# A 32-byte load from each row of the first block of b, put first on ScalarE's queue

## The chip, the cores and the metric

The kernel runs on one core of one Trainium2 chip. The metric is the device time of one execution in microseconds (us); the number given is the median over several runs. Five engines work side by side: TensorE (PE in the profile; PEld is its loading of weights), VectorE (DVE), ScalarE (ACT), GpSimd (POOL) and SyncE (SP). DMAs are issued by SP, ACT or POOL and carried out by 16 DMA engines.

## The reference

```python
def reference(a, b, c):            # a 1024x1024, b 1024x2048, c 2048x1024, float32
    h = np.matmul(a, b)
    h = 0.5 * h * (1 + np.tanh(np.sqrt(2 / np.pi) * (h + 0.044715 * h ** 3)))
    return np.matmul(h, c).astype(np.float32)
```

Two matrix products with a GELU (tanh form) between them.

## The kernel before

All loads are started at the beginning, and the whole schedule is written out by hand: each engine carries out its instructions in the order of the program text, and a tile's readers wait for its writers.

The first product needs `a` transposed. Parts of `a` and `b` come in two ways. SP's queue loads five pieces as float32 into staging tiles (`sta` for a, `stb` for b), lines 75 to 79; DVE and ACT then cast them to bf16 (`cast_a`, `cast_b`, lines 108 and 110). All the rest is loaded by POOL's queue, which casts on the way, lines 86 to 104. POOL's first load stands behind a small copy (line 81) that reads the first piece of `a`, so that it isn't issued before that piece has landed.

The five pieces on SP's queue, in order:

- line 75, `a_part(0, 0)`: rows 0 to 511 of a, columns 0 to 255, 512 KB, as 512 runs of 1,024 bytes. In what follows, a(0,0).
- line 76, `b_part(0)`: rows 0 to 255 of b, columns 0 to 511, 512 KB, as 256 runs of 2,048 bytes. Partition p gets row p and row p + 128. In what follows, b(0).
- line 77, `a_part(1, 0)`: rows 512 to 1023 of a, columns 0 to 255, 512 KB: a(1,0).
- line 78, `a_part(0, 1)`: rows 0 to 511 of a, columns 256 to 511, 512 KB: a(0,1).
- line 79: rows 256 to 383 of b, columns 0 to 511, 256 KB.

A row of b has 2,048 floats, so rows that follow each other lie 8 KB apart in memory; a row of a has 4 KB.

ScalarE's first work is a GELU on one column (line 82), which loads its function table. PE starts with products on a constant (`stir`, line 125), then turns the pieces of `a` with transposes (line 145, copied out by DVE in line 146 into `aT`), and computes the first 512 columns of h with plain products, block by block as the pieces arrive (`block`, line 114). While a(0,0) and b(0) are worked on, a(1,0) has to land, and so on.

From 24 us on, the other columns of h and the second product are made by the class `Seven`: a 2x2 scheme of Strassen and Winograd with seven products in place of eight (line 212), whose sums of operands are made by DVE (line 170) and whose results are collected by ACT (line 298) and DVE (line 303). The outputs are stored from SP's queue (line 429).

The tile `room`, 16 floats a partition, is allocated in line 55 and not used.

Of the kernel before, what the change touches and what calls it, by code (L numbers as in the profile page):

```python
# [9 lines left out]
F32 = mybir.dt.float32  # L10
# [9 lines left out]
def kernel(ctx, tc, a, b, c, out):  # L20
    nc = tc.nc
# [8 lines left out]
    bv = b.rearrange("(kt p) n -> p kt n", p=128)  # L30
# [3 lines left out]
    consts = ctx.enter_context(tc.tile_pool(name="consts", bufs=1))  # L34
# [17 lines left out]
    gate = consts.tile([128, 1], F32, name="gate")  # L52
    g = consts.tile([128, 1], F32, name="g")

    consts.tile([128, 16], F32, name="room")

    c_sb = keep.tile([128, NT, P], BF16, name="c_sb")
    hT = [keep.tile([128, NT, H], BF16, name=f"hT{h}") for h in range(2)]
# [10 lines left out]
    def a_part(h, q):  # L69
        return av[:, 4 * h:4 * h + 4, ds(q * 256, 256)]  # L70

    def b_part(q):
        return bv[:, 2 * q:2 * q + 2, 0:H]

    nc.sync.dma_start(out=sta[:, 0, 0], in_=a_part(0, 0))  # L75
    nc.sync.dma_start(out=stb[:, 0:2], in_=b_part(0))  # L76
    nc.sync.dma_start(out=sta[:, 1, 0], in_=a_part(1, 0))
# [21 lines left out]
    for n in range(2):  # L99
        for k in range(0, KT, 4):  # L100
            nc.gpsimd.dma_start(out=b2[:, k:k + 4, ts(n, H)],
                                in_=bv[:, k:k + 4, ds(1024 + n * H, H)])
# [385 lines left out]
```

## Time and profile before

| | us |
|---|---|
| median of 3 runs | 117.6 (117.41 to 117.97) |
| span of the profiled execution, first to last instruction | 115.7 |
| PE busy in it | 111.1 |
| DVE busy | 90.0 |
| ACT busy | 51.4 |

The profile is of one execution. Its span leaves out what lies before the first and after the last instruction; the time of a run has it in, which is why the median is 1.9 us longer than the span. The granted clock of TensorE was 1.00 throughout.

The DMA queues in the whole execution (packets, megabytes, and share of the time of the 16 engines): the rows of the queue that SP issues on (q1) and of POOL's (q0).

```profile
q0 software_dynamic: 8672, 9.31, 47.6%
q1 hardware_dynamic: 4736, 6.56, 15.8%
```

The issues on SP's queue at the start, from the timeline (start, length of the issue, queue, line, what is loaded). The length is the time that SP needs to issue, not the time of the transfer:

```profile
1.24 0.50 SPq L76 DMA_DIRECT2D stb<-in_b_dram  x1
1.78 0.46 SPq L77 DMA_DIRECT2D sta<-in_a_dram  x1
2.29 0.51 SPq L78 DMA_DIRECT2D sta<-in_a_dram  x1
2.83 0.55 SPq L79 DMA_DIRECT2D stb<-in_b_dram  x1
```

From issue to landing these loads take (median of each kind) 6.1 us for the three of `sta` and 5.3 us for line 76.

### The profile page before, as it was taken

Reading aid. Unit: us, or ns where it says so; the run is one execution under the profiler, and the core shown is the slowest. Engines: PE = TensorE matmul, PEld = TensorE weight load, DVE = VectorE, ACT = ScalarE, POOL = GpSimd, SP = SyncE. Lnnn points to the kernel's source line nnn. Section 1 sums busy time; section 2 is a strip of 40 time slices with the busy share of each in tenths; the row PEclk is TensorE's granted clock in tenths of the full one; section 3 lists DMA queues with packets and bytes.
Section 4 is the critical chain, followed back from the end, with each engine's and each line's share of the span. In section 5 each row is a group of like instructions: output and inputs, shape, how many; then the busy total and the mean of one; then the engine's idle time right before and its main releaser. Section 6 shows DMA issues by size and latency. Waiting matters only on the chain.

```text
span 115.7 us, 1461 instructions
## 1 busy us (share of the span) xinstructions
PE 111.1 (96%) x542; PEld 77.1 (67%) x542; DVE 90.0 (78%) x107; ACT 51.4 (44%) x86; POOL 17.2 (15%) x29
## 2 busy tenths in 40 slices
PE   7989999999999999999999999999999999999980
PEld 6645555546776447888885444688888888888860
DVE  0347748789999998935699999999999986954770
ACT  5053000999259997166698429500124982000000
POOL 2497755223322000000000000000000000000000
PEclk9999999999999999999999999999999999999999
DMA  2999999999999999998000000060000002014993
GB/s 69 295 381 229 200 199 205 204 208 205 206 211 209 212 213 209 212 210 168 8 0 0 6 0 0 38 235 0 0 0 0 0 4 91 1 73 176 370 363 106
DMA packets 13414, 15.94 MB, mean 138 GB/s; under 512 B 736, under 2 KB 9312, under 8 KB 13408
## 3 DMA queue, kind: packets, MB, share of 16 engines
q0 software_dynamic: 8672, 9.31, 47.6%
q1 hardware_dynamic: 4736, 6.56, 15.8%
q8 instruction: 4, 0.07, 0.3%
q14 instruction: 2, 0.02, 0.0%
HBM read 20.97 MB, written 4.19 MB: 218 GB/s over the span
## 4 chain that ended last, share of the span: by engine, by line
PE 90%; DMA 5%; SPq 1%; DVE 1%; issue 0%
PE ps L212 76%; PE ps L114 11%; DMA sta<-in_a_dram 5%; PE pt L145 3%; SPq L76 0%; DVE ab L110 0%; SPq L75 0%; DVE ot L375 0%
## 5 line engine op out<-in xcount | busy, mean ns | idle before, releaser
L212 PE MATMUL ps<-x,s 128*128 128x512 f32 x128 | 29.6, 391 | 0.0
L212 PEld LDWEIGHTS ps<-x,s 128*128 128x128 f32 x128 | 24.0, 188 | 5.1
L212 PE MATMUL ps<-x,x 128*128 128x512 f32 x96 | 22.9, 394 | 0.0
L212 PEld LDWEIGHTS ps<-x,x 128*128 128x128 f32 x96 | 18.0, 188 | 3.9
L114 PE MATMUL ps<-aT,b 128*128 128x512 bf16 x64 | 16.1, 379 | 0.2 <-DVE b L110 0.2
L298 ACT ACTIVATE v<-ps 128x512 f32<-128x512 f32 x10 | 6.0, 599 | 19.1 <-PE ps L212 19.1
L212 PE MATMUL ps<-c_sb,hT 128*128 128x512 bf16 (+1 forms) x72 | 14.2, 356 | 0.0
L212 PE MATMUL ps<-x 128*128 128x512 f32 x56 | 13.2, 392 | 0.0
L212 PEld LDWEIGHTS ps<-x 128*128 128x128 f32 x56 | 10.2, 188 | 2.6 <-ACT u L298 0.4
L118 ACT ACTIVATE hT<-ps 128x512 bf16<-128x512 f32 x14 | 7.3, 595 | 9.7 <-PE ps L114 9.7
L212 PEld LDWEIGHTS <-hT 128*128 128x128 bf16 x72 | 6.9, 98 | 7.0 <-issue 0.5
L118 ACT ACTIVATE hT<-ot 128x512 bf16<-128x512 f32 x18 | 10.4, 624 | 2.0 <-DVE ot L303 2.0
L212 PE MATMUL ps<-aT,b 128*128 128x512 bf16 x48 | 10.7, 379 | 0.0
L146 DVE COPY aT<-pt 128x512 bf16<-128x512 bf16 x16 | 6.7, 423 | 5.1 <-PE pt L145 5.1
L303 DVE TENSOR_TENSOR ot<-ps,u 128x512 f32<-128x512 f32 x10 | 6.7, 690 | 5.1 <-ACT u L298 5.1
L303 DVE TENSOR_TENSOR ot<-ps,v 128x512 f32<-128x512 f32 x10 | 6.7, 688 | 4.8 <-DMA out_dram<-ot 3.8
L170 DVE TENSOR_TENSOR x<-c_sb 128x1024 fp32r<-128x1024 bf16 x8 | 9.3, 1226 | 0.0
L114 PEld LDWEIGHTS <-b 128*128 128x128 bf16 x64 | 5.7, 98 | 4.5 <-DVE b L110 0.3
L212 PEld LDWEIGHTS <-b 128*128 128x128 bf16 x48 | 4.6, 98 | 5.7 <-issue 0.3
L104 POOL DMA_DIRECT2D c_sb<-in_c_dram x8 | 5.6, 702 | 13.1 <-DMA b<-in_b_dram 12.4
L170 DVE TENSOR_TENSOR x<-b 128x1024 fp32r<-128x1024 bf16 (+1 forms) x4 | 7.0, 1752 | 0.6 <-issue 0.6
L298 ACT ACTIVATE u<-ps 128x512 f32<-128x512 f32 x10 | 5.9, 598 | 3.4 <-PE ps L212 3.2
(44 smaller groups left out, 111.3 us busy)
## 6 DMA issues: line engine op xcount, KB each, us to landing
c_sb<-in_c_dram POOLq DMA_DIRECT2D x8, 512.0 KB, 20.0
out_dram<-ot SPq DMA_DIRECT2D x13, 256.0 KB, 2.1
b<-in_b_dram POOLq DMA_DIRECT2D x6, 512.0 KB, 15.3
sta<-in_a_dram SPq DMA_DIRECT2D x3, 512.0 KB, 6.1
abq<-in_a_dram POOLq DMA_DIRECT2D x5, 256.0 KB, 7.9
out_dram<-ot SPq DMA_DIRECT2D x6, 128.0 KB, 2.0
stb<-in_b_dram SPq DMA_DIRECT2D x1, 512.0 KB, 5.3
b<-in_b_dram POOLq DMA_DIRECT2D x2, 256.0 KB, 8.2
```

The costliest lines, as they stand in the source:

```text
L104: nc.gpsimd.dma_start(out=c_sb[:, t:t + 2], in_=cv[:, t:t + 2])
L114: nc.tensor.matmul(p, b1[:, k, ts(t, 128)], aT[:, h, k], start=(k == 0), stop=(k == KT - 1))
L118: nc.scalar.activation(hT[h][:, t], p, AF.Gelu_apprx_tanh)
L145: nc.tensor.transpose(pt[:, n, ts(m, 128)], ab[:, m, ts(n, 128)], ident)
L146: nc.vector.tensor_copy(aT[:, h, 2 * q + n], pt[:, n])
L170: nc.vector.tensor_tensor(out=dst[:, r], in0=x[:, r], in1=y[:, r], op=op)
L212: nc.tensor.matmul(p[:, ds(c0, w)], l[:, k, ts(j, 128)], r[:, k, ds(c0, w)], start=(start and k == 0), stop=(k == self.kt - 1), skip_group ...
L298: nc.scalar.activation(st, p, AF.Copy)
L303: nc.vector.tensor_tensor(out=ot, in0=p, in1=st, op=ADD)
```

## The change

`room` gets a name and the shape 128 x 2 x 8 in place of 128 x 16, the same 64 bytes a partition. One DMA is added ahead of the five on SP's queue in the text, on ScalarE's queue, where it is the first instruction. It reads the first 8 floats (32 bytes) of each of the rows 0 to 255 of b, partition p getting rows p and p + 128 as in `b_part(0)`. No instruction reads `room`. All other instructions stay as they are, in the same order on each engine; their line numbers go up by one.

```diff
-    consts.tile([128, 16], F32, name="room")
+    room = consts.tile([128, 2, 8], F32, name="room")
...
+    nc.scalar.dma_start(out=room, in_=bv[:, 0:2, 0:8])
     nc.sync.dma_start(out=sta[:, 0, 0], in_=a_part(0, 0))
     nc.sync.dma_start(out=stb[:, 0:2], in_=b_part(0))
     nc.sync.dma_start(out=sta[:, 1, 0], in_=a_part(1, 0))
```

## The prediction

> **What bounds the kernel now.** I read the chain of waits first, then its first 13 us piece by piece, then the timeline and a table by stretches of the same time, and last the single packets of the DMA queues.
>
> ```profile
> span 115.7 us, 1461 instructions
> PE 111.1 (96%) x542; PEld 77.1 (67%) x542; DVE 90.0 (78%) x107; ACT 51.4 (44%) x86; POOL 17.2 (15%) x29
> PE 90%; DMA 5%; SPq 1%; DVE 1%; issue 0%
> ```
>
> TensorE sets the end: 90% of the chain is PE, and PE runs from 8.38 us to 112.4 us with no gap. The only other large piece is a load, 5% of the span, and it lies at the start:
>
> ```profile
> 0.74 0.44 SPq L75
> 1.24 0.50 SPq L76
> 1.78 6.10 DMA sta<-in_a_dram
> 7.90 0.44 DVE ab L110
> 8.38 0.62 PE pt L145 x8
> ```
>
> This load is the third one on SP's queue, line 77 (I call it a(1,0)). It lands at 7.88 us; DVE and ACT cast it, PE turns it, and from there PE never stops. So the end stands at "landing of a(1,0)" plus work that does not depend on the change. The load waits 6.10 us because two others are ahead of it in the DMA engines: a(0,0) of line 75 and b(0) of line 76. That is where the change acts.
>
> ```profile
> 0.74 1.28 ACT L82 ACT_TABLE_LOAD   x1 [0.74 <-PEq L472]
> 2.03 0.20 ACT L82 ACTIVATE g<-const-float32-0.0 128x1 f32<-128x1 f32 x1
> 4.40 0.69 DVE L110 CAST ab<-sta 128x1024 bf16<-128x1024 f32 x1 [4.40 <-DMA sta<-in_a_dram]
> 6.54 0.94 ACT L108 ACTIVATE b<-stb 128x256 bf16<-128x256 f32 x2 [4.30 <-DMA stb<-in_b_dram]
> 7.90 0.43 DVE L110 CAST ab<-sta 128x512 bf16<-128x512 f32 x1 [0.67 <-DMA sta<-in_a_dram]
> ```
>
> The casts start when the loads land: a(0,0) at 4.38, b(0) at 6.51, a(1,0) at 7.88 us. Each load has 512 KB. b(0) takes 6.51 - 4.38 = 2.13 us, a(1,0) only 1.37 us. The table of stretches (columns: the stretch, its length, busy time of the five engines, granted clock, DMA share, GB/s) says the same:
>
> ```profile
> 0.00:1.85 1.85, 1.07 (x3) 0.92 (x4) 0.00 (x0) 1.11 (x1) 0.69 (x6) 1.00 0.00 1
> 1.85:3.60 1.75, 1.75 (x6) 1.39 (x5) 0.00 (x0) 0.38 (x2) 0.00 (x0) 1.00 0.83 262
> 3.60:5.60 2.00, 1.93 (x11) 1.34 (x10) 0.71 (x2) 0.00 (x0) 1.17 (x2) 1.00 0.91 265
> 5.60:7.10 1.50, 1.11 (x10) 0.76 (x10) 0.97 (x4) 0.56 (x2) 1.50 (x3) 1.00 1.07 363
> 7.10:8.40 1.30, 1.21 (x7) 0.36 (x6) 0.56 (x2) 0.87 (x2) 1.30 (x3) 1.00 1.09 386
> 8.40:9.20 0.80, 0.80 (x10) 0.64 (x11) 0.38 (x2) 0.13 (x1) 0.80 (x2) 1.00 1.07 378
> ```
>
> 265 GB/s while b(0) is read, 386 GB/s later, on the same queue. In the trace's packet records b(0) has 256 packets of 2,048 bytes, of mean length 114 ns, 86 of them stretched (over 92 ns, up to 405 ns). The 128 packets of the next load from b, line 79, take 84 ns each without one exception. b(0)'s excess over 84 ns is 7.8 us in all, 0.49 us for each of 16 engines. a(0,0) shows 34 stretched packets of 512 (2.8 us, 0.17 us an engine), a(1,0) shows 3. Between 5.6 and 5.85 us b(0)'s last packets are still stretched (187, 153, 145 ns) while a(1,0)'s beside them on other engines all take 46 ns. So the stretching belongs to b(0), not to that moment.
>
> **The change part by part.** Added: one DMA on ScalarE's queue, 128 x 2 x 8 floats, 256 pieces of 32 bytes from the rows that b(0) reads, with no reader. Nothing is removed. All else keeps its order on PE, DVE, POOL and SP; the tile `room` has the 64 bytes a partition that it had.
>
> Gain S, what b(0) saves. Lower bound 0: the touch warms nothing. Upper bound: b(0) runs at a(1,0)'s pace, 2.13 - 1.37 = 0.76 us. What decides is why b(0) is slow. For "first touch of this part of b": the clean next load from b has the same pitch of 8 KB between rows, and POOL's later loads of pairs of rows of b, which move 2,048 bytes read per 98 ns packet, show one slightly stretched packet among 810. Neither pitch nor pairs alone are slow later. Against it: lines 77 and 79 also touch new rows and are clean, so the cold thing must be larger than a row. With the touch in the same order, the engine that reads a row later touches it first, so I take the upper bound, S = 0.76.
>
> Cost T, the engines' time for the touch. 256 pieces over 16 engines are 16 packets each and one semaphore packet. No 32-byte packet is in the trace; the nearest row is the 4-byte semaphore packet of 9 ns, so 17 x 9 = 0.15 us an engine. Upper bound: all of b(0)'s excess moves into the touch, 0.15 + 0.49 = 0.64 us. Lower bound 0, since the engines are not full while a(0,0) begins: from 1.85 to 2.5 us 82 packets start, where 16 engines at a(1,0)'s pace (1.37 us for 32 packets each) would start 0.65 x 16 x 32 / 1.37 = 243; two thirds of 0.65 us, 0.43 us an engine, is empty. The touch is issued at the same moment as a(0,0) and falls into that hole. I take the middle of 0 and 0.15, T = 0.07; the cover is this hole, and without it T is 0.15 to 0.64.
>
> Cost D, a later first issue on SP. ACT and SP both start at 0.74 us. An issue on SP takes 0.44 to 0.55 us here. If the two don't share anything, or SP comes first, D = 0: b(0)'s own issue at 1.24 is over long before its first packet at 3.59 us, so half a microsecond there is hidden. If ACT's comes first and SP's must wait, a(0,0) and all behind it move by D = 0.44. The trace shows no two queues issuing at once. I take 0, and keep 0.44 for the range.
>
> The Trainium skill speaks against this: "Perfetto Trace Analysis", section "DMA Instruction — HWDGE (DVE, Sync)", says that the block that writes the descriptors is shared by two sequencers and locked by one at a time. No row here shows it; by that rule, with ScalarE first, D would be the 0.44 and my sum 117.35.
>
> ScalarE itself: the issue (0.44 to 0.55, as on SP) goes ahead of the table load of 1.28 us and the activation of 0.20 us, which then end near 2.8 instead of 2.23 us. ScalarE's next work is the cast of b at 6.54, or 5.8 if b(0) is faster; 3 us of idle time hide this. What would be late next without that cover is this cast, and PE's first products at 6.83 us.
>
> What follows behind a(1,0): a(0,1) and the last part of b are behind it on the same queue and move with it. POOL's queue comes next: its first DMA was issued at 5.08 to 5.95, but its packets begin at 9.01 us, and they begin engine by engine (3, 5, 22, 33 packets in the four tenths of a microsecond from 9.0), as the last packets of SP's queue leave (8.95 to 9.6 us). So it starts when SP's queue is drained, and moves too. If it didn't, PE would soon wait: the half of `abq` that lands at 15.84 is used at 16.09, so only 0.25 us of a gain would stay.
>
> Before b(0): if a(0,0) lands a little later by T, its cast (4.40 to 5.09), PE's turns (5.15) and DVE's copy (to 6.00) still end near b(0)'s new landing, 5.8; a(1,0) would land at 7.2 and still be last.
>
> Sum: -S + T + D = -0.76 + 0.07 + 0 = -0.69 us. The profiled execution has a span of 115.7 us; the median of the runs is 117.6 us, 1.9 us more, which lies around the span and which I leave as it is. So a span near 115.0, and 117.6 - 0.7 = 116.9 us.
>
> **The rivals.**
>
> (1) The stall only moves. The 256 touches pay what b(0) paid, ahead of a(0,0): T = 0.64, so -0.76 + 0.64 = -0.12, 117.5 us. For it: 0.49 us an engine has to be paid somewhere, if it is paid by row. Against it: the empty time in a(0,0)'s start, and the clean new rows of lines 77 and 79.
>
> (2) Slower: the stretch is not a matter of first touch. b(0)'s rows then read as slowly after the touch (S = 0), and the touch, on the same rows, stands ahead of a(0,0) with T = 0.15 to 0.64; in the middle 0.40, 118.0 us, and with D = 0.44 118.4 us. It decides from the point where T + D is more than S, that is, when less than T + D of the 0.76 us is saved. For it: the touch reads 32 of 2,048 bytes, and rows that lines 77 and 79 read for the first time are not slow at all. Against it: b's later loads are clean.
>
> (3) The gain is hidden: S is had, but POOL's queue starts by its own clock, and PE waits for `abq`: 0.25 us remain, 117.35 us. Against it: the hand-over engine by engine.
>
> **How the numbers follow.** The forecast has 0.48 (own range 116.6 to 117.3, from S = 0.76 with T up to 0.15, down by a tenth or two for what a(0,0) itself may save of its 0.17, up for a part of S), (1) 0.17, (2) 0.28, (3) 0.07. A measurement of this kernel can tell about 0.5%, 0.59 us, from no change: faster is below 117.0, slower above 118.2. Of the forecast 0.35 lie below 117.0, the rest above; (1) and (3) are within. Of (2) about 0.2 lie above 118.2 (with D, or with T near 0.64), the rest below; 0.06 more I give to slowdowns where (1) comes with D and with stretched packets in a(0,0). So faster 0.35, same 0.39, slower 0.26. The range goes from 116.6 to 118.4: below it lies S and all of a(0,0)'s stretching, above it more than T = 0.40 with D.
>
> **What would show it.** Right: b(0)'s packets at 84 ns, the casts on `stb` near 5.8 us, the one on `sta` that starts PE near 7.2 us, POOL's first packets near 8.3 us, and the rest of PE moved as one block. S is wrong if b(0)'s packets keep a mean near 114 ns. T is wrong if a(0,0) lands well after 4.45 us though its first packet starts at 1.85; D is wrong if that first packet, or SP's first issue, comes 0.4 us later. The whole is wrong if PE has new gaps between 12 and 22 us, where it waits for `abq` or `b`.

## The result and the profile after

The changed kernel takes 118.09 us (median of 16 runs, 117.97 to 118.66) against 117.58 us for the kernel before in the same comparison (16 runs, 117.40 to 118.10): a ratio of 1.0043, 95% interval 1.0031 to 1.0055. The change costs half a microsecond; the forecast was a gain of 0.7. Each ratio and interval here and below is taken over the runs without those that took over 1.5% longer than the fastest of their kernel, so it need not be the ratio of the two medians.

The page of the changed kernel shows the new load as a queue of its own, with 272 packets (256 of data and 16 that report the end):

```profile
span 116.2 us, 1462 instructions
q10 hardware_dynamic: 272, 0.01, 0.1%
```

The timeline of its start, the rows that answer to those shown of the kernel before (line numbers are one higher):

```profile
0.74 0.49 ACTq L75 DMA_DIRECT2D room<-in_b_dram  x1
0.74 0.42 SPq L76 DMA_DIRECT2D sta<-in_a_dram  x1
1.26 1.28 ACT L83 ACT_TABLE_LOAD   x1 [1.26 <-PEq L473]
4.56 0.69 DVE L111 CAST ab<-sta 128x1024 bf16<-128x1024 f32 x1 [4.56 <-DMA sta<-in_a_dram]
6.54 0.94 ACT L109 ACTIVATE b<-stb 128x256 bf16<-128x256 f32 x2 [3.78 <-DMA stb<-in_b_dram]
8.02 0.43 DVE L111 CAST ab<-sta 128x512 bf16<-128x512 f32 x1 [0.75 <-DMA sta<-in_a_dram]
```

The casts of a(0,0) start 0.16 us later than before (4.56 against 4.40), those of b(0) at the very same 6.54, those of a(1,0) 0.12 us later. So b(0) did not become faster: in the packet records its 256 packets have a mean of 115 ns (114 before), 79 of them stretched (86 before). Yet the touch's own 256 packets take 9 ns each, none stretched. In the table of stretches b(0)'s two microseconds (from 3.6 to 5.6) show 277 GB/s in place of 265, with the touch's last packets and a(0,0)'s among them:

```profile
3.60:5.60 2.00, 2.00 (x8) 1.18 (x7) 0.69 (x1) 0.00 (x0) 1.01 (x2) 1.00 0.97 277
7.10:8.40 1.30, 1.23 (x6) 0.38 (x4) 0.55 (x2) 0.75 (x2) 1.30 (x3) 1.00 1.09 386
```

The chain of waits of the changed kernel, from a(1,0) to the end of the computation:

```profile
1.77 6.23 DMA sta<-in_a_dram
8.02 0.44 DVE ab L111
8.51 0.62 PE pt L146 x8
9.13 1.10 PE ps L115 x5
...
24.58 87.94 PE ps L213 x400
112.54 0.42 DVE ot L376
```

Its last pieces in the kernel before:

```profile
24.46 87.96 PE ps L212 x400
112.44 0.42 DVE ot L375
```

PE's unbroken run begins at 8.51 us instead of 8.38 (+0.13), and DVE's last addition begins at 112.54 us; before, it began at 112.44 (+0.10). But the span grew by 0.53 us (115.67 to 116.20). Most of the loss, then, comes after the last addition, where the prediction did not look at all. There, SP stores the last piece of the output and then waits for every DMA to be reported. The waits of SP in the last 5 us, first of the kernel before, then of the changed one (what waited, for what, us in total, times, the longest):

```profile
SPq L483 <- DMA out_dram<-ot: 1.1, 2, 0.8
SPq L483 <- PEq L483: 0.6, 2, 0.5
```

```profile
SPq L484 <- DMA out_dram<-ot: 1.5, 1, 1.5
SPq L484 <- PEq L484: 0.6, 2, 0.5
```

Before, SP waited twice for stores: for the last but one, then for the last. After, it waited once, for 1.5 us. The trace's semaphore records show the order of this list (us, and the two semaphores that each instruction waits for; the last store is reported on the one marked *):

```
before                        after
113.27  115 114               113.37  116 115
113.34  102 113               114.91  100* 114
113.41  103 112               114.97  102 113
113.47  104 111               115.04  104 112
113.53  106 110               115.10  105 111
113.59  107 109               115.16  107 110
113.65  116 108               115.22  108 109
113.93  117 105               115.28  117 106
114.79  118* 100              115.34  118 103
114.92  SP done               115.46  SP done
```

The loads and stores of SP and ACT report on eight semaphores, taken in turn. Before, these were 102, 103, 104, 106, 107, 116, 117, 118; the 24 DMAs are three full turns, so the last store has the eighth, and SP waits for that one last. All other waits of the list are done while the store is still under way. In the changed kernel there are 25 DMAs. The touch, first on ScalarE's queue, took the first (100), all others moved on by one, and the last store has the first again. SP waits for it second of nine, and the seven waits that follow, long fulfilled, still cost 0.06 us each. From the landing of the last store to the end of the span: 114.78 to 115.67 = 0.89 us before, 114.89 to 116.20 = 1.31 us after.

So the 0.53 us of the span are 0.11 us up to the last landing and 0.42 us behind it.

### The profile page after: what moved, and what is told of

Read it like the earlier page. It is cut to its first block, busy times and chain, and to the rows that moved or that the text cites. A ratio compares the mean times of both kernels' runs of the same rounds, so it can differ in the third digit from the quotient of the medians.

```text
span 116.2 us, 1462 instructions
## 1 busy us (share of the span) xinstructions
PE 111.5 (96%) x542; PEld 77.5 (67%) x542; DVE 89.9 (77%) x107; ACT 51.3 (44%) x86; POOL 17.3 (15%) x29
## 4 chain that ended last, share of the span: by engine, by line
PE 90%; DMA 5%; SPq 1%; DVE 1%; issue 0%
PE ps L213 76%; PE ps L115 11%; DMA sta<-in_a_dram 5%; PE pt L146 3%; SPq L77 0%; DVE ab L111 0%; DVE ot L376 0%; SPq L76 0%
```

## The experiments

The theory, T (in the expectations "Theory T"; not the prediction's cost T of the touch): the loss is the list of waits at the end, since the number of DMAs on SP and ACT went from 24 to 25; the touch itself costs next to nothing and warms nothing. The first rival, R1: the loss lies at the start. Apart from that stands the question why b(0) is read slowly.

### The touch without the twenty-fifth DMA

```diff
 # the changed kernel
-        n = 2 if (i, l) == (0, 0) and j else 1
+        n = 2 if (i, l) == (0, 0) and j > 1 else 1
```

> The touch stays, but one store in the middle of the output (tile row 1) goes out as one piece of 512 columns in place of two of 256, so that SP and ACT issue 24 DMAs as in the kernel before, not 25. Theory T (the final chain of waits): the 8 completion semaphores are given out in turn, so the last store is on the eighth again, which SP waits for last at the end; the 0.43 us between the landing of the last store and the end that the touch had added is gone, and only the 0.13 us by which PE starts later stays: 117.7 us, 1.001 of before; from the landing of the last store to the end 0.9 us. Rival R1 (the touch costs its time at the start, and the rest is drift of PE): still about 118.1, 1.004. Rival R2 (the merged store itself changes the time): anything else.

Measured: 117.69 us (12 runs, 117.46 to 118.35) against 117.51, ratio 1.0014, interval 0.9999 to 1.0028. From the last landing to the end 0.89 us, as in the kernel before. The waits of SP at the end are again two, as before the change:

```profile
SPq L484 <- DMA out_dram<-ot: 1.1, 2, 0.8
```

With the touch in place and the last store back on the eighth semaphore, the loss is gone but for 0.14%, which can't be told from nothing. (The execution that was profiled is one of the longer of the twelve, 118.20 us: PE's unbroken run begins at 9.14 us in it. It shows the end of the kernel, not the size of the effect.)

### The twenty-fifth DMA without the touch

The first try cuts one store of the output in two, in the kernel before:

```diff
-        n = 2 if (i, l) == (0, 0) and j else 1
+        n = 2 if (i, l) == (0, 0) else 1
```

> No touch; the kernel before with one store in the middle of the output (tile row 0) sent as two pieces of 256 columns in place of one of 512, which makes 25 DMAs on SP and ACT. Theory T: the last store is on the first of the 8 semaphores, which SP waits for second of 9 pairs; seven more pairs at 0.062 us each follow after it has landed: +0.43 us, 118.0 us, 1.0037 of before, though the loads and PE's start are as before (8.38 us). Rival R1: 117.6, no change.

Measured: 118.46 us (5 runs, 118.21 to 118.57), 1.0073 of before, interval 1.0057 to 1.0089: more than T says. The end is as T says, 1.31 us from the last landing to the end of the span. In the profiled execution (118.57 us, the longest of the five) the rest lies at the start. Its chain of waits:

```profile
1.77 6.76 DMA sta<-in_a_dram
8.56 0.44 DVE ab L110
...
9.04 0.62 PE pt L145 x8
```

PE begins at 9.04 us, 0.66 later than before: one of the 16 engines finished its share of b(0) at 7.17 us where the next slowest needed until 6.41, with one packet of 769 ns. Nothing in the edit touches these loads. The run supports T in its end and is of no use for the size. Why b(0) was late in this kernel's runs stayed open.

So the twenty-fifth DMA was made in another way: the touch itself, but issued in the middle of the kernel.

```diff
 # the kernel before
-    consts.tile([128, 16], F32, name="room")
+    room = consts.tile([128, 2, 8], F32, name="room")
...
     seven(one, done1, between1)
+    nc.scalar.dma_start(out=room, in_=bv[:, 0:2, 0:8])
```

> No touch at the start; the same 32-byte load of 256 rows of b is issued on ScalarE's queue between the second and the third product stage (near 60 us), where the loads are long over. 25 DMAs on SP and ACT as in the change. Theory T (the chain of waits at the end): from the landing of the last store to the end 1.3 us in place of 0.9, so 118.0 us, 1.0037 of before, with PE starting at 8.4 us as before. Rival R1 (the whole cost of the change lies at its start): 117.6, 1.000.

Measured: 118.05 us (12 runs, 117.87 to 118.73) against 117.57, ratio 1.0042, interval 1.0023 to 1.0061: the loss of the change, with nothing altered at the start. The waits of SP at the end are those of the changed kernel, while DVE's last addition begins at 112.48 us, within 0.04 us of the kernel before:

```profile
SPq L484 <- DMA out_dram<-ot: 1.5, 1, 1.5
```

R1 falls.

### The control for the merged store

The kernel before with the store merged as in the first run (23 DMAs, the last store on the seventh semaphore).

> No touch; the kernel before with the store of tile row 1 in one piece, 23 DMAs on SP and ACT. It is the control for the merged store of the run with the touch and 24 DMAs. Theory T: the last store is on the seventh semaphore, and one more pair of waits (0.06 us) follows its landing: 117.65, between 1.000 and 1.001 of before. Rival R2 (merging the store is worth time by itself): below 0.998.

Measured: 117.69 us (11 runs, 117.45 to 117.93) against 117.57, ratio 0.9995, interval 0.9971 to 1.0019; from the last landing to the end 0.95 us, one wait more than in the kernel before. Merging the store is worth nothing that can be told here (the interval reaches from -0.34 to +0.22 us). With and without the touch, the medians are the same 117.69 us, though in two comparisons in which the kernel before had 117.51 and 117.57 us.

All runs of this kind in one table (a wait here is one instruction of the list, carried out from the last landing on):

| kernel | DMAs on SP and ACT | waits from the last landing on | last landing to end, us | ratio to before |
|---|---|---|---|---|
| before | 24 | 1 | 0.89 | 1 |
| the change | 25 | 8 | 1.31 | 1.0043 |
| touch, 24 DMAs | 24 | 1 | 0.89 | 1.0014 |
| one store cut in two | 25 | 8 | 1.31 | 1.0073 |
| touch in the middle | 25 | 8 | 1.31 | 1.0042 |
| one store merged | 23 | 2 | 0.95 | 0.9995 |

Seven waits more are 0.42 us, one more is 0.06 us.

### Did the touch come too late?

In the changed kernel the touch's packets run from 2.56 to 3.93 us, side by side with a(0,0)'s, and b(0) begins at 3.63 us. So the warming could have been right and only too late. Two runs hold all loads back by 4.4 us with work of DVE on the staging tile; the second has the touch at the beginning as well.

```diff
 # the kernel before; the second run: the changed kernel, with the same line behind the touch
+    nc.vector.memset(sta, 0.0)
     nc.sync.dma_start(out=sta[:, 0, 0], in_=a_part(0, 0))
```

> No touch; DVE first clears the staging tile sta (4,096 floats a partition, some 4 us), and SP's loads wait for that, so that all loads begin some 4 us later. Theory L (the slow reading belongs to the first microseconds after the launch): b(0)'s packets then have a mean near 84 ns. Theory B (it belongs to b(0) or to its place behind a(0,0)): the mean stays over 105 ns. Time some 4 us longer in both, near 121.7.

> As the run with late loads, with the touch on ScalarE's queue at the beginning as in the change: the touch is over some 2 us before a(0,0) is read. Theory W (the touch warms, but in the change it came too late): b(0)'s packets have a mean near 84 ns, where the run with late loads alone has over 105. Theory N (a touch of 32 bytes a row does nothing for the later reading): the same mean as in the run with late loads alone, within 10 ns, and the touch's own packets near 9 ns.

Measured: without the touch b(0)'s packets have a mean of 122 ns, with it 128 ns, and the touch's own take 8 to 9 ns. The touch was over at 2.12 us and b(0) began at 7.95 us. Two rows of the table of stretches, most of b(0) and the beginning of a(1,0), first without the touch, then with it:

```profile
8.00:10.00 2.00, 0.38 (x4) 0.38 (x5) 0.69 (x1) 0.00 (x0) 1.09 (x2) 0.72 1.04 286
10.00:11.60 1.60, 1.60 (x12) 1.35 (x10) 1.02 (x4) 0.69 (x2) 1.60 (x3) 0.50 1.07 373
```

```profile
8.00:10.00 2.00, 0.50 (x5) 0.50 (x5) 0.69 (x1) 0.00 (x0) 1.21 (x2) 0.50 1.01 270
10.00:11.60 1.60, 1.60 (x10) 1.22 (x9) 1.00 (x4) 0.58 (x2) 1.60 (x4) 0.50 1.06 367
```

The last column: 270 GB/s for b(0) and 367 behind it, though the touch was over nearly six microseconds before; without the touch 286 and 373. Theory N: the touch does nothing for the later reading. Nor is b(0) clean when it is read 4.4 us later, so the first microseconds after the launch are not the reason. The times of these two, 123.9 and 123.5 us, are 2 us longer than expected; PE had nothing to do while it waited for the loads, and its granted clock was 0.50 at the start of the work (the column ahead of the last two), so they are of use for the packets only.

Then the whole of b(0), all 2,048 bytes of each row, read ahead in place of 32:

```diff
 # the kernel before
+    nc.scalar.dma_start(out=stb[:, 4:6], in_=b_part(0))
+    nc.vector.memset(sta, 0.0)
     nc.sync.dma_start(out=sta[:, 0, 0], in_=a_part(0, 0))
```

> As the run with late loads, with a reading of all 2,048 bytes of each of b(0)'s rows (into a part of the staging tile that nobody reads) on ScalarE's queue at the beginning, over before a(0,0) is read. Theory F (first touch matters, at a grain finer than 32 bytes a row): b(0)'s second reading has a mean near 84 ns, the first near 114 ns or more. Theory P (b(0)'s pattern or place makes it slow each time): both means over 105 ns.

Measured: the first reading has a mean of 108 ns, the second, of the same bytes and begun 3.6 us after the end of the first, 115.5 ns with 94 stretched packets. Theory P: having been read 3.6 us before does not make b(0) faster, and this holds for whole rows as for 32 bytes of each. (These are single executions; in the profiled executions of the six kernels that load b(0) in second place, without a hold and from its own rows, the mean lies between 113 and 134 ns.)

### What makes b(0) slow?

Five runs tried to find it; they narrow it down and don't settle it.

Read twice in a row, ahead of all other loads:

```diff
 # the kernel before, row 1 stored in one piece (as in the two kernels below that cut b(0) in two, so that 24 DMAs stay)
+    nc.sync.dma_start(out=stb[:, 4:6], in_=b_part(0))
     nc.sync.dma_start(out=sta[:, 0, 0], in_=a_part(0, 0))
```

> No touch; ahead of all other loads SP loads the whole of b(0), 2,048 bytes a row, into a part of the staging tile that nobody reads, and then a(0,0), b(0) and the rest as before (24 DMAs, row 1 stored in one piece). Theory P (b(0) is slow by the pattern or place of its reads, each time): the second reading has stretched packets as the first, mean over 105 ns. Rival C (first touch, at a grain finer than 32 bytes a row): the first reading has a mean near 114 ns or more, the second 84 ns. In both the time is about 1.4 to 2.1 us longer, near 119.3.

Measured: the first reading 143 ns (75 stretched, up to 884 ns). The second: 84 ns in each of its first two quarters, 84.5 in the third, 119 in the last, 93 in all. Neither theory holds as it was put: less than a full repetition, and not clean. Time 120.16 us. Taken alone this run spoke for first touch; the run above, with an idle stretch between the two readings, speaks against it. The two differ in the pause: here the second reading begins 0.9 us after the end of the first, there 3.6 us. That a reading of whole rows helps one that follows at once, and no longer after some microseconds, fits both and was not tested.

Other rows of b:

```diff
-    nc.sync.dma_start(out=stb[:, 0:2], in_=b_part(0))
+    nc.sync.dma_start(out=stb[:, 0:2], in_=b_part(2))
```

> No touch; in place of b(0)'s rows 0 to 255 the same load reads rows 512 to 767 of b (so the product uses other rows of b for the first two steps of K). Theory R (rows 0 to 255 are special, or slow since they are the first of b): if the place in the order counts, a mean over 105 ns again; if only rows 0 to 255 are slow, 84 ns. Time near 117.6 or 116.9.

Measured: 122 ns, 89 stretched packets, 118.08 us (one run). The rows 0 to 255 are not special.

Cut by rows, and cut by columns:

```diff
-    nc.sync.dma_start(out=stb[:, 0:2], in_=b_part(0))
+    nc.sync.dma_start(out=stb[:, 0], in_=bv[:, 0, 0:H])
+    nc.sync.dma_start(out=stb[:, 1], in_=bv[:, 1, 0:H])
```

> No touch; b(0) is loaded as two DMAs of one row a partition (rows 0 to 127, then 128 to 255) in place of one DMA of pairs of rows (24 DMAs, row 1 stored in one piece). Theory P1 (the alternation of two rows 1 MB apart makes b(0) slow): packets of both at 84 ns, a(1,0) lands 0.7 us earlier, time 116.9. Rival C (first reads from b are slow): the packets keep a mean over 105 ns at least in the first half, time 117.4 to 117.7. Rival P2 (b(0)'s place in time, behind a(0,0)): both halves stretched, 117.6.

Measured: 119.12 us (6 runs, 117.97 to 119.34), ratio 1.0105, interval 1.0068 to 1.0142. In the profiled execution, the longest of the six, the packets have a mean of 159 ns, up to 1,316 ns. The alternation of two rows is not the cause: without it the reading was slower still in this execution.

```diff
-    nc.sync.dma_start(out=stb[:, 0:2], in_=b_part(0))
+    nc.sync.dma_start(out=stb[:, 0:2, 0:256], in_=bv[:, 0:2, 0:256])
+    nc.sync.dma_start(out=stb[:, 0:2, 256:], in_=bv[:, 0:2, 256:H])
```

> No touch; b(0) as two DMAs of 256 columns each (runs of 1,024 bytes as in the loads of a) in place of one of 512 columns; row 1 stored in one piece, 24 DMAs. If the length of the runs makes the reading slow: packets near 46 ns, the two halves take 1.4 us in all and the time falls towards 116.9. If first reading is slow whatever the shape: stretched packets in the first half at least, time 117.6 or more, as when b(0) was cut by rows.

Measured: 118.78 us (8 runs, 118.10 to 120.78), ratio 1.0078, interval 1.0031 to 1.0126. In order of start and 128 at a time, the first 256 packets behind a(0,0) have means of 46 and 51 ns, the next 384 of 80, 74 and 68 ns. The slow stretch has moved back, it has not gone.

Last, a version that was to beat both kernels: b(0) loaded third, with a(1,0)'s cast and transposes ahead of all products.

```diff
-    nc.sync.dma_start(out=stb[:, 0:2], in_=b_part(0))
     nc.sync.dma_start(out=sta[:, 1, 0], in_=a_part(1, 0))
+    nc.sync.dma_start(out=stb[:, 0:2], in_=b_part(0))
...
     stir(128)
-    cast_b(0, nc.vector, nc.vector, nc.scalar)
     next(tn)
     stir(64)
-    cast_b(1, nc.scalar)
     ab = cast_a(1, 0, nc.vector, nc.scalar)
-    block(0, range(4), (0,))
-    block(0, range(2), (1,))
     for _ in turn(1, 0, (7, 6), ab):
         pass
-    block(0, range(2, 4), (1,))
+    cast_b(0, nc.vector, nc.vector, nc.scalar)
+    cast_b(1, nc.scalar)
+    block(0, range(4), (0, 1))
```

> No touch, 24 DMAs; b(0) is loaded third, behind a(1,0), and the cast and the transposes of a(1,0) go ahead of b's casts and of all products of the first block. If a load of b(0)'s shape is slow only as one of the first two in a stream: packets near 84 ns, b(0) lands near 7.2 us, the eight first products and eight transposes are done some 0.3 us earlier than before (9.2 in place of 9.4 us), 117.3 us. If it is slow here too (mean over 105 ns): b(0) lands near 7.9 us, and the time is 117.9 or more.

Measured: 120.94 us (6 runs, 120.56 to 122.34), ratio 1.0299, interval 1.0254 to 1.0344. In the third place, too, b(0)'s packets have a mean of 123 ns; it landed at 8.74 us, and a(1,0) in the second place was clean (46 ns a packet). So PE got its first products later than expected, and its clock made it worse: busy for only 1.51 of the 3.05 us from 6.00 on, it was granted half of the clock soon after. Of this run, three rows of the table of stretches (the column ahead of the last two is the granted clock):

```profile
6.00:9.05 3.05, 1.51 (x16) 0.99 (x16) 2.07 (x7) 0.57 (x2) 3.05 (x5) 1.00 0.97 295
9.50:12.90 3.40, 3.40 (x9) 1.20 (x10) 0.81 (x2) 1.34 (x4) 1.65 (x3) 0.50 1.36 215
12.90:16.00 3.10, 3.05 (x24) 1.76 (x24) 1.73 (x4) 0.00 (x0) 2.02 (x4) 1.00 1.38 198
```

Nine matmuls in 3.4 us at 0.50, 24 matmuls and transposes in 3.1 us at 1.00. (In the changed kernel's chain five such products take 1.10 us at full clock, so nine would take 2.0; some 1.4 us are lost here.) No version that was run beats the kernel before.

What these runs show of b(0): the load is slow as the first, the second and the third of the stream, with other rows, with single rows, with shorter runs, early and late, and 3.6 us after the same bytes were read. The one reading that was clean for three quarters is the one that began 0.9 us after another of the same rows. The load that ends SP's five, 128 rows of the same pitch and length (line 79 before the change), keeps a mean of 84 to 88.5 ns in all runs. Its shape is not the difference: the two halves of b(0) that were cut by rows have the same shape and were slow (in order of start, a mean of 210 and of 108 ns). What is different about the two was not found.

## Why the prediction was wrong, point by point

**S, what b(0) saves: this step failed.** The prediction took the upper bound, S = 0.76 us, "for 'first touch of this part of b'". The measured S is 0: 115 ns a packet after the change (114 before it), 128 ns when the touch had ended 5.8 us before (122 without it), 115.5 ns when all the bytes had been read 3.6 us before. Why b(0) is read slowly stays open. The prediction had evidence against it in hand when it set down that lines 77 and 79 read new rows with hardly a stretched packet (3 of 512 and none of 128); it set that aside by supposing that the cold thing is "larger than a row". The reason given for this, that neither pitch nor pairs are slow later, excluded two causes and left more than one.

**A term that was missing: the end of the kernel.** The prediction puts the end at "landing of a(1,0)" plus work that the change leaves alone, and counts the DMA's packets, its issue, and its neighbours in the queues. It doesn't count that each DMA of SP and ACT takes the next of eight semaphores. The one that was added moved the last store from the last wait of SP's list to the second, 7 x 0.06 = 0.42 us, four fifths of the loss in the span. The touch in the middle of the kernel gave the same ratio (1.0042) with DVE's last addition within 0.04 us of the kernel before, and the touch with 24 DMAs gave 1.0014.

**T, the engines' time for the touch: the packets' length was right, the cover was not.** The packets took 9 ns, as the 4-byte row said, so 0.15 us an engine. The prediction took 0.07, half of it hidden in the hole from 1.85 to 2.5 us. But the touch's first packet came at 2.56 us, when the hole was over, and its packets ran among a(0,0)'s. In the profiled runs a(0,0) lands 0.16 us and a(1,0) 0.12 us later than before; over all runs, the touch with 24 DMAs gives between 0 and 0.33 us (interval 0.9999 to 1.0028), and the medians with and without it, with the merged store, are equal. One profiled execution can't weigh a tenth of a microsecond here: without any touch PE began at 8.38 us in the kernel before and at 9.04 us in another with the same loads.

**D, a later first issue on SP: right.** SP's first issue stands at 0.74 us with 0.42 us, its first packet at 1.85 us, both as before. The touch was the one that waited: its first packet comes at 2.56 us, but at 1.79 us in the run where SP's queue was still quiet; of this wait little shows in ScalarE's issue, 0.49 against 0.41 us. Of the section "DMA Instruction — HWDGE (DVE, Sync)" of the Trainium skill's "Perfetto Trace Analysis", which has the sequencers take turns at one block, these 0.77 us between the two may be the trace. It agrees in kind and doesn't prove it: the touch could as well have waited in the engines behind a(0,0). That ScalarE would come first was not so.

**ScalarE and what follows.** The table load ended at 2.54 and the activation at 2.76 us, near the 2.8 of the prediction, and ScalarE was idle for 3.78 us behind it: hidden, as said. That POOL's queue starts as SP's is drained, and with it the third rival, was not put to the test, since SP's queue didn't get shorter. The runs at hand agree with it: in the kernels with b(0) cut by rows and with b(0) third, POOL's first issue stands at 4.94 and 4.97 us, but its first packet at 9.39 and 8.87 us, shortly before the first engine ended its part of SP's five loads at 9.65 and 8.95 us.

**The rivals.** The second one, "the stretch is not a matter of first touch", was right that S = 0, and its reason is the better supported one, though a help of whole rows read directly ahead stays open. It named 118.0 us, but by a cost that isn't there: it put the loss of 0.40 us into the touch's packets ahead of a(0,0). The agreement of its number with the measured 118.09 us is chance. That the stall moves from b(0) into the touch (the first rival) is excluded: b(0)'s packets kept theirs (115 ns), and the touch's took 9 ns each.

## What to carry to other kernels

An added or removed DMA changes more than its own queue: where completion semaphores are given out in turn and the kernel ends with a list of waits, count the DMAs, and let the last store report on the semaphore that is waited for last; here a place near the head of the list costs 0.42 us, four fifths of what the change lost. Look at the stretch from the last landing to the end of the span in every comparison of kernels whose difference is under one per cent. And before a load is "warmed", read the same bytes twice, once with a pause between and once without, and see whether the second reading is any faster.

## What was not expected of the hardware

- A wait that is long fulfilled still costs: nine instructions of SP, two semaphores each, follow each other at 0.06 us (113.27, 113.34, 113.41, ...).
- Reading the same 512 KB again 3.6 us later was not faster (115.5 ns a packet after 108).
- Packets of 32 bytes took 9 ns, as did those of 4 bytes, and came interleaved with the 1,024-byte packets of the other queue: from 2.7 to 3.5 us between 17 and 35 of the touch beside 19 to 32 of a(0,0) in each tenth of a microsecond. "DMA: Bandwidth & Descriptors", section "Queues, rings and completion order", of the Trainium skill has each engine go round its queues and change over between packets; a packet there is a bundle of several descriptors (orders to move one run of bytes), not the single run that the trace's records count. This run agrees that the two queues take turns; the grain at which one engine changes over it does not show, since these counts are of all 16 engines together.
- With PE idle for half of the three microseconds from 6.00 to 9.05 us, one kernel was granted half the clock from 9.50 to 12.90 us.
